# Softmax of a banded attention with negated scores, scales on ScalarE, one reciprocal for three tiles, and convolution taps ordered behind the minima

## The chip, the cores and the metric

One core of a Trainium2 chip runs the kernel. Its engines work side by side, each with a queue of its own that it works off in order: TensorE (PE, matrix products and transposes), VectorE (DVE), ScalarE (ACT), GpSimd (POOL) and SyncE (SP), which issues most of the DMAs. Semaphores between the queues say when an instruction may start. The metric is the time of the whole program on the device in microseconds, as the median of several executions.

## The reference

One layer of a streaming encoder, for 2048 prompt tokens and 64 sample tokens, with a model width of 1024 and 8 heads of 64:

```python
h = rms_norm(x, norm1_g) * (1 + sc1) + sh1
z = h @ w_in                          # GLU pair | q | k | v | two gates
u = glu_a * sigmoid(glu_b)
conv_out = conv_module(u, ...)        # depthwise conv of 31 taps, layer norm, swish, product
q, k = rms_norm(q), rms_norm(k)       # per head
s = einsum('bqhd,bkhd->bhqk', q, k) * 0.125 + rel_bias
s = where(mask, s, NEG_INF)           # own chunk of 64 and the 8 chunks before
o = einsum('bhqk,bkhd->bqhd', softmax(s, axis=-1), v)
merged = sigmoid(g_conv) * conv_out + sigmoid(g_attn) * (o @ w_attn_out)
x = x + gt1 * (merged @ w_o)
x = x + gt2 * swiglu_ffn(rms_norm(x, norm2_g) * (1 + sc2) + sh2)
```

The cached rows of the sample's keys, values and convolution inputs are read, and their new states are outputs. All is in float32.

## The kernel before

Float32 products are made of three products of parts: an operand is split into a high and a low part (whi and wlo for weights, hh and hl for activations, ph and pl for probabilities), so a row ps<-hh,whi is followed by ps<-hl,whi and ps<-hh,wlo.

The program has two phases. In phase 1 the 2112 tokens go through in four blocks (576 with the samples, then three of 512). Each block goes through the stages q, 0, k, 1, v, 2, 3 and g: projections to queries, keys and values; four stages of the GLU pair with the convolution of 128 channels each (`convolve`, L1158, whose 30 taps are a `scalar_tensor_tensor` each on VectorE, L1174, y<-u,wd,y in the rows); and the gates. The attention of a block needs its v, and runs beside the stages that follow: those of its own block and the first of the next one. Phase 2 (from about 1230 us) makes the gated merge, the output projection and the FFN in three blocks of tokens.

Attention works head by head (`attend`, L1371), 40 in all: 16 in block 0 (eight of the prompt, with four tiles of 128 queries and 128, 256, 384 and 512 keys, and between them eight of the samples, with one tile of 64 x 320), and eight in each later block, with four tiles of 128 x 640. Per tile: TensorE makes the scores into sc, of which there is one buffer in PSUM. `softmax_max` (L1270) adds the bias, multiplies by 0.125 and takes the maximum of each row, in one instruction on VectorE (in the order a row ISA pr,sm and a row ISA sm, in the trace CUSTOM_DVE_ANT_0 and its accumulator read), negates the maximum on VectorE, and ScalarE makes Exp with the sum. `softmax_scale` (L1285) takes the reciprocal on VectorE and multiplies the tile by it: on VectorE in blocks 0 to 2, on ScalarE in block 3 (`ON_ACT = (3,)`, L48). It is called for a tile when the next one's Exp has been written down. When all four are scaled, TensorE transposes the probabilities (ptp), ScalarE and VectorE split them into ph and pl, and TensorE multiplies them by the values into po; `finish_head` (L1313) adds two halves into o_p.

What sets the order: the code is written as generators on `Lane`s (L109), which a `Stream` (L162) steps on as TensorE's estimated load passes the time that each has asked for, as long as the load of VectorE and ScalarE isn't too far ahead:

```python
stream.lanes = [norm_lane, work, attn, tail, conv]    # L1476
yield free + PE_LAG, SCORE_ROOM                       # L1396, between two tiles
yield stream.when("act" if x in ON_ACT else "dve") + PE_LAG   # L1404, before the transposes
```

Behind that the compiler's own scheduler sorts the instructions once more by its estimates, so that the final order on an engine is not the order of the code. The operations of all engines go through one recording helper, so nearly all rows have its line (L104 before, L103 after); they are told apart by their tiles.

Of the kernel before, what the change touches and what calls it, by code (L numbers as in the profile page):

```python
# [8 lines left out]
F32 = mybir.dt.float32  # L9
F32R = mybir.dt.float32r  # L10
AF = mybir.ActivationFunctionType
ALU = mybir.AluOpType
# [4 lines left out]
P = 128  # L17
# [26 lines left out]
PE_LAG = 400.0  # L44
TURN_LAG = 2500.0
KN_LAG = 5000.0
X_LAG = 8000.0
ON_ACT = (3,)  # L48
ON_POOL = ()
# [8 lines left out]
SCORE_ROOM = {"dve": 2500}  # L58
# [525 lines left out]
def streaming_layer(ctx: ExitStack, tc: tile.TileContext, I, O):  # L584
    nc = tc.nc
    stream = Stream()
    pe, dve, act, gps = (
        Meter(e, n, stream) for e, n in ((nc.tensor, "pe"), (nc.vector, "dve"), (nc.scalar, "act"), (nc.gpsimd, "pool"))
    )
# [44 lines left out]
    wd = const.tile([P, 4, TAPS], F32, name="wd")  # L634
# [91 lines left out]
    wk = p1.enter_context(tc.tile_pool(name="wk", bufs=1))  # L726
# [201 lines left out]
    bias = wk.tile([P, 640], F32, name="bias")  # L928
# [203 lines left out]
    def glu(b, ct):  # L1132
# [23 lines left out]
        return u  # L1156

    def convolve(u, y, ct, b):  # L1158
        w = UW if b == 0 else HIST + QB
        n = w - HIST  # L1160
# [12 lines left out]
        for k in range(1, TAPS):  # L1173
            dve.scalar_tensor_tensor(y[:, ct, :n], u[:, k : k + n], wd[:, ct, k : k + 1], y[:, ct, :n], ALU.mult, ALU.add)  # L1174
            yield
# [93 lines left out]

    def softmax_max(ps, n, w, bias):  # L1270
        pr = wk.tile([P, 640], F32, tag="pr", name="pr", bufs=8)
        sm = wk.tile([P, 4], F32, tag="sm", name="sm", bufs=9)
        nb = ps.shape[1]
        stream.after("dve", "pe")
        dve.tensor_tensor_reduce(
            out=pr[:n, :w].rearrange("p (a b) -> p a b", a=nb), in0=ps, in1=bias.rearrange("p (a b) -> p a b", a=nb),
            scale=0.125, scalar=-3e38, op0=ALU.add, op1=ALU.max, accum_out=sm[:n, 0:1],
        )
        dve.tensor_scalar(sm[:n, 1:2], sm[:n, 0:1], -1.0, None, ALU.mult)
        free = stream.when("dve")  # L1280
        stream.after("act", "dve")
        act.activation(pr[:n, :w], pr[:n, :w], AF.Exp, bias=sm[:n, 1:2], accum_out=sm[:n, 2:3])
        return pr, sm, free, stream.when("act")

    def softmax_scale(pr, sm, n, w, on_act):  # L1285
        dve.reciprocal(sm[:n, 3:4], sm[:n, 2:3])
        if on_act:
            stream.after("act", "dve")
            act.activation(pr[:n, :w], pr[:n, :w], AF.Copy, scale=sm[:n, 3:4])
        else:  # L1290
            dve.tensor_scalar(pr[:n, :w], pr[:n, :w], sm[:n, 3:4], None, ALU.mult)

# [55 lines left out]

    order, loaded, now = [], {}, {"scored": -1, "finished": -1, "bias": None}

# [20 lines left out]
    def attend(i):  # L1371
        x, h = order[i]
        q0, nq, k0, nk = spans(x)
# [4 lines left out]
        (q2, kk), (_, bias), vnow = now["qk", i], now["bias"], now["v", i]  # L1378
        tiles = []
        for t in range(0, nq, P):  # L1380
            n = min(P, nq - t)
# [6 lines left out]
            else:  # L1388
# [3 lines left out]
                src, bs = ps[:n, 0:1, :w], bias[:n, 64:384][:, ::-1] if x == "s" else bias[:, :w][:, ::-1]  # L1392
            pr, sm, free, ready = softmax_max(src, n, w, bs)
            tiles.append((pr, sm, n, w))
            if t + P < nq:
                yield free + PE_LAG, SCORE_ROOM  # L1396
            else:
                fetch(i + 1)
                now["scored"] = i
            if t:  # L1400
                softmax_scale(*tiles[-2], x in ON_ACT)
        yield ready
        softmax_scale(*tiles[-1], x in ON_ACT)
        yield stream.when("act" if x in ON_ACT else "dve") + PE_LAG  # L1404
        while now["finished"] < i - 1:
# [676 lines left out]
```

## Time and profile before

| | us |
|---|---|
| median of three executions | 3047.6 (3043.95 to 3049.64) |
| the profiled execution | 3048.7 |
| its span, first to last instruction | 3046.9 |
| TensorE busy | 2936.2 |
| VectorE busy | 2043.0 |
| ScalarE busy | 1254.4 |
| GpSimd busy | 989.7 |
| mean granted TensorE clock | 0.987 |

In the rows, "out<-in" names tiles of the program and "x" the number of instructions in a row. In a timeline a row starts with its start and its length in us, and "[5.64 <-DVE sm]" is idle time of that engine ahead of it and what ended it. In a table of windows each engine's busy time stands before its number of instructions. In the groups of instructions "busy, mean ns of one" is followed by the idle time of the engine ahead of them. In the rows of waits the numbers are the total in us, how many, and the longest.

### The profile page before, as it was taken

How to read it: one execution, taken by the hardware profiler on the slowest of the kernel's cores; microseconds unless marked ns; L12 is line 12 of the kernel's file. 1: busy time of each engine (PE TensorE's matmuls, PEld its weight loads, DVE VectorE, ACT ScalarE, POOL GpSimd, SP SyncE). 2: the span in 40 equal slices, each digit the busy share in tenths (PEclk: the TensorE clock that was granted, in tenths of full speed). 3: DMA queues.
4: the chain of work that ended last, by engine and by line, in shares of the span. 5: the costliest groups of instructions: out<-in, count | busy, mean ns of one | idle time of the engine just before them, and what ended most of it. 6: DMA issues, size and time to landing. Idle time of an engine off the chain costs nothing. (4 is left out here: it accounts for less than half of the span.)

```text
span 3046.9 us, 44878 instructions
## 1 busy us (share of the span) xinstructions
PE 2936.2 (96%) x16259; PEld 2609.2 (86%) x16259; DVE 2043.0 (67%) x3826; ACT 1254.4 (41%) x2260; POOL 989.7 (32%) x617
## 2 busy tenths in 40 slices
PE   7989898999999999989999999999999999999998
PEld 4789777888878788878998989999999898999997
DVE  4797687877977895467666755655666756366567
ACT  2324432453245257364444424534444244333331
POOL 0200210101011102355677433247767341333331
PEclk9999998999999999999999999999999999999999
DMA  9789788887987788886444686445556965355554
GB/s 336 262 276 309 224 293 267 270 263 265 306 277 247 250 267 274 259 278 218 144 149 142 227 292 202 159 166 190 181 196 202 344 213 189 119 167 174 166 162 174
DMA packets 487084, 693.07 MB, mean 227 GB/s; under 512 B 38485, under 2 KB 316873, under 8 KB 486862
## 3 DMA queue, kind: packets, MB, share of 16 engines
q1 hardware_dynamic: 474581, 672.82, 67.2%
q10 hardware_dynamic: 12280, 17.39, 1.6%
q8 instruction: 128, 2.10, 0.3%
q14 instruction: 95, 0.77, 0.1%
HBM read 505.89 MB, written 184.19 MB: 226 GB/s over the span
## 5 line engine op out<-in xcount | busy, mean ns | idle before, releaser
L104 POOL TENSOR_TENSOR wlo<-wst,whi 128x1024 fp32r<-128x1024 f32 (+1 forms) x180 | 402.6, 2243 | 499.5 <-ACT whi L104 427.6
L104 PE MATMUL ps<-t,whi 128*128 128x384 f32 (+1 forms) x2112 | 505.8, 323 | 10.5 <-DVE t L104 4.8
L104 PE MATMUL pd<-whi,hid 128*128 128x512 f32 (+1 forms) x1400 | 450.3, 391 | 3.4 <-DVE acc L104 3.4
L104 ACT ACTIVATE whi<-wst 128x1024 fp32r<-128x1024 f32 (+1 forms) x269 | 262.0, 978 | 360.5 <-PE ps L104 120.1
L104 PE MATMUL ps<-b,whi 128*128 128x384 f32 (+1 forms) x1584 | 381.1, 326 | 11.4 <-DVE pw L104 4.0
L104 PEld LDWEIGHTS ps<-t,whi 128*128 128x128 f32 x2112 | 370.6, 189 | 18.6 <-ACT u L104 5.5
L104 DVE SCALAR_TENSOR_TENSOR y<-u,wd,y 128x512 f32<-128x512 f32 (+1 forms) x480 | 368.3, 771 | 6.5
L104 PE MATMUL ps<-hh,whi 128*128 128x512 f32 (+2 forms) x992 | 363.6, 367 | 0.0
L104 PE MATMUL ps<-hl,whi 128*128 128x512 f32 (+2 forms) x992 | 346.6, 349 | 0.0
L104 PE MATMUL ps<-hh,wlo 128*128 128x512 f32 (+2 forms) x992 | 346.0, 349 | 0.0
L104 DVE TENSOR_TENSOR acc<-acc,pd 128x512 f32<-128x512 f32 (+1 forms) x440 | 290.5, 684 | 80.4 <-PE pd L104 76.8
L104 PE MATMUL ps<-t,wlo 128*128 128x384 f32 (+1 forms) x1056 | 340.8, 323 | 0.0
L104 PEld LDWEIGHTS pd<-whi,hid 128*128 128x128 f32 (+1 forms) x1400 | 258.1, 184 | 64.7 <-DVE acc L104 6.9
L104 PEld LDWEIGHTS ps<-b,whi 128*128 128x128 f32 x1584 | 278.1, 189 | 14.7 <-DVE pw L104 4.3
L104 PE MATMUL pd<-wlo,hid 128*128 128x512 f32 (+1 forms) x700 | 273.7, 391 | 0.0
L104 PE MATMUL ps<-b,wlo 128*128 128x384 f32 (+1 forms) x792 | 257.1, 325 | 0.0
L104 POOL TENSOR_TENSOR r<-t,mhalf 128x8 f32<-128x8 f32 (+3 forms) x68 | 84.5, 1244 | 390.9 <-DVE t L104 368.0
L104 PEld LDWEIGHTS ps<-hh,wlo 128*128 128x128 f32 x992 | 187.9, 189 | 22.4
L104 POOL TENSOR_TENSOR wlo<-wup,whi 128x1024 fp32r<-128x1024 f32 (+1 forms) x64 | 138.3, 2162 | 208.8 <-ACT whi L104 176.5
L104 PEld LDWEIGHTS ps<-hh,whi 128*128 128x128 f32 x992 | 188.8, 190 | 18.7 <-issue 2.1
L104 PEld LDWEIGHTS ps<-hl,whi 128*128 128x128 f32 x992 | 188.8, 190 | 15.4 <-issue 1.7
L104 PEld LDWEIGHTS ps<-t,wlo 128*128 128x128 f32 x1056 | 199.3, 189 | 0.6
(217 smaller groups left out, 5725.5 us busy)
## 6 DMA issues: line engine op xcount, KB each, us to landing
whi<-w_din_h SPq DMA_DIRECT2D x72, 512.0 KB, 5.9
wlo<-w_din_l SPq DMA_DIRECT2D x72, 512.0 KB, 7.1
wst<-sum_d SPq DMA_DIRECT2D x131, 256.0 KB, 3.0
wmod<-in_w_ada SPq DMA_DIRECT2D x48, 512.0 KB, 8.5
sum_d<-ws SPq DMA_DIRECT2D x88, 256.0 KB, 2.4
wst<-in_w_ffn_in SPq DMA_DIRECT2D x85, 256.0 KB, 3.4
wst<-in_w_ffn_in SPq DMA_DIRECT2D x37, 512.0 KB, 5.4
wst<-in_w_in SPq DMA_DIRECT2D x36, 512.0 KB, 7.1
```

Source lines behind the costliest of these rows:

```text
L104: return f(*args, **kw)
```

## The change

Scores are kept negated: the scale is -0.125, the tile's extreme is a minimum, and Exp takes its input times -1 with the minimum as its bias, so that the separate negation is gone. The bias is added as before. One tile sm of 128 x 12 per head replaces one of 128 x 4 per tile of scores. The scale of every tile is a Copy on ScalarE; those of the first three tiles are written behind the fourth Exp, with one reciprocal over three columns, and the last has a reciprocal of its own; a sample head has one. The first tap that is written after a minimum is tied behind it on VectorE (`behind`, which uses the scheduler's `issue_after`).

```diff
@@ -1,4 +1,4 @@
-from contextlib import ExitStack
+from contextlib import ExitStack, nullcontext
 
 import concourse.bass as bass
 import concourse.tile as tile
@@ -45,7 +45,6 @@
 TURN_LAG = 2500.0
 KN_LAG = 5000.0
 X_LAG = 8000.0
-ON_ACT = (3,)
 ON_POOL = ()
 DMA_LAG = 4000.0
 OUT_LAG = 4000.0
@@ -1155,6 +1154,12 @@
         W.done()
         return u
 
+    def behind(one):
+
+        return tc.issue_after(one.ins) if one is not None else nullcontext()
+
+    now = {"scored": -1, "finished": -1, "bias": None}
+
     def convolve(u, y, ct, b):
         w = UW if b == 0 else HIST + QB
         n = w - HIST
@@ -1171,7 +1176,8 @@
         gps.tensor_copy(hist[:, ct], u[:, w - HIST : w])
         dve.tensor_scalar(y[:, ct, :n], u[:, :n], wd[:, ct, 0:1], bdw[:, ct : ct + 1], ALU.mult, ALU.add)
         for k in range(1, TAPS):
-            dve.scalar_tensor_tensor(y[:, ct, :n], u[:, k : k + n], wd[:, ct, k : k + 1], y[:, ct, :n], ALU.mult, ALU.add)
+            with behind(now.pop("least", None)):
+                dve.scalar_tensor_tensor(y[:, ct, :n], u[:, k : k + n], wd[:, ct, k : k + 1], y[:, ct, :n], ALU.mult, ALU.add)
             yield
 
     def conv_norm(y, c0, n, t0):
@@ -1267,28 +1273,29 @@
             free["columns"] = c1
 
 
-    def softmax_max(ps, n, w, bias):
+    def softmax_max(ps, n, w, bias, sm, j):
+
         pr = wk.tile([P, 640], F32, tag="pr", name="pr", bufs=8)
-        sm = wk.tile([P, 4], F32, tag="sm", name="sm", bufs=9)
         nb = ps.shape[1]
         stream.after("dve", "pe")
-        dve.tensor_tensor_reduce(
+        now["least"] = dve.tensor_tensor_reduce(
             out=pr[:n, :w].rearrange("p (a b) -> p a b", a=nb), in0=ps, in1=bias.rearrange("p (a b) -> p a b", a=nb),
-            scale=0.125, scalar=-3e38, op0=ALU.add, op1=ALU.max, accum_out=sm[:n, 0:1],
+            scale=-0.125, scalar=3e38, op0=ALU.add, op1=ALU.min, accum_out=sm[:n, j : j + 1],
         )
-        dve.tensor_scalar(sm[:n, 1:2], sm[:n, 0:1], -1.0, None, ALU.mult)
         free = stream.when("dve")
         stream.after("act", "dve")
-        act.activation(pr[:n, :w], pr[:n, :w], AF.Exp, bias=sm[:n, 1:2], accum_out=sm[:n, 2:3])
-        return pr, sm, free, stream.when("act")
-
-    def softmax_scale(pr, sm, n, w, on_act):
-        dve.reciprocal(sm[:n, 3:4], sm[:n, 2:3])
-        if on_act:
-            stream.after("act", "dve")
-            act.activation(pr[:n, :w], pr[:n, :w], AF.Copy, scale=sm[:n, 3:4])
-        else:
-            dve.tensor_scalar(pr[:n, :w], pr[:n, :w], sm[:n, 3:4], None, ALU.mult)
+        act.activation(pr[:n, :w], pr[:n, :w], AF.Exp, bias=sm[:n, j : j + 1], scale=-1.0, accum_out=sm[:n, 4 + j : 5 + j])
+        return pr, n, w
+
+    def softmax_scale(tiles, sm, a, b):
+
+        n = tiles[a][1]
+        stream.after("dve", "act")
+        dve.reciprocal(sm[:n, 8 + a : 8 + b], sm[:n, 4 + a : 4 + b])
+        stream.after("act", "dve")
+        for j in range(a, b):
+            pr, n, w = tiles[j]
+            act.activation(pr[:n, :w], pr[:n, :w], AF.Copy, scale=sm[:n, 8 + j : 9 + j])
 
     def load_qk(h, q0, nq, k0, nk):
         hp, i = divmod(h, 2)
@@ -1346,7 +1353,7 @@
             )
         return bias
 
-    order, loaded, now = [], {}, {"scored": -1, "finished": -1, "bias": None}
+    order, loaded = [], {}
 
     def attention(b):
 
@@ -1376,7 +1383,8 @@
         fetch_v(i)
         yield loaded[i]
         (q2, kk), (_, bias), vnow = now["qk", i], now["bias"], now["v", i]
-        tiles = []
+        tiles, nt = [], (nq + P - 1) // P
+        sm = wk.tile([P, 12], F32, tag="sm", name="sm", bufs=3)
         for t in range(0, nq, P):
             n = min(P, nq - t)
             ps = ps_a.tile([P, 2, 512], F32, tag="s", name="sc")
@@ -1390,18 +1398,17 @@
                 for d in range(2):
                     pe.matmul(ps[:n, 0, :w], q2[:, d, t : t + n], kk[:, :w], start=d == 0, stop=d == 1)
                 src, bs = ps[:n, 0:1, :w], bias[:n, 64:384][:, ::-1] if x == "s" else bias[:, :w][:, ::-1]
-            pr, sm, free, ready = softmax_max(src, n, w, bs)
-            tiles.append((pr, sm, n, w))
+            tiles.append(softmax_max(src, n, w, bs, sm, t // P))
             if t + P < nq:
-                yield free + PE_LAG, SCORE_ROOM
+                yield stream.when("dve") + PE_LAG, SCORE_ROOM
             else:
                 fetch(i + 1)
                 now["scored"] = i
-            if t:
-                softmax_scale(*tiles[-2], x in ON_ACT)
-        yield ready
-        softmax_scale(*tiles[-1], x in ON_ACT)
-        yield stream.when("act" if x in ON_ACT else "dve") + PE_LAG
+        if nt > 2:
+            softmax_scale(tiles, sm, 0, nt - 1)
+        yield stream.when("act")
+        softmax_scale(tiles, sm, nt - 1 if nt > 2 else 0, nt)
+        yield stream.when("act") + PE_LAG
         while now["finished"] < i - 1:
             yield lambda: now["finished"] == i - 1
         fetch_v(i + 1)
```

In instructions: VectorE loses 136 negations, 104 scales and 64 reciprocals and gains three wlo that GpSimd loses; ScalarE gains 104 Copies; the counts on TensorE and SyncE are the same. The order on every engine is the same up to the first head of attention and from the first rows of phase 2 on. Between them it differs at many places. Three follow.

VectorE at the first head of attention, before (y<-u,wd,y are taps, ISA pr,sm the tile with its maximum, sm<-sm the negation):

```order
L104 SCALAR_TENSOR_TENSOR y<-u,wd,y 128x606
L104 TENSOR_SCALAR cc<-pt 30x128
L104 SCALAR_TENSOR_TENSOR y<-u,wd,y 128x606 x5
L104 ISA pr,sm<-sc,bias 128x128
L104 ISA sm 128x1
L104 SCALAR_TENSOR_TENSOR y<-u,wd,y 128x606
L104 TENSOR_SCALAR sm<-sm 128x1
L104 ISA pr,sm<-sc,bias 128x256
L104 ISA sm 128x1
L104 SCALAR_TENSOR_TENSOR y<-u,wd,y 128x606
L104 TENSOR_SCALAR sm<-sm 128x1
L104 RECIPROCAL sm<-sm 128x1
```

and after:

```order
L103 TENSOR_SCALAR cc<-pt 30x128
L103 ISA pr,sm<-sc,bias 128x128
L103 ISA sm 128x1
L103 SCALAR_TENSOR_TENSOR y<-u,wd,y 128x606
L103 ISA pr,sm<-sc,bias 128x256
L103 ISA sm 128x1
L103 SCALAR_TENSOR_TENSOR y<-u,wd,y 128x606
L103 ISA pr,sm<-sc,bias 128x384
L103 ISA sm 128x1
L103 SCALAR_TENSOR_TENSOR y<-u,wd,y 128x606
L103 ISA pr,sm<-sc,bias 128x512
L103 ISA sm 128x1
```

The five taps ahead of the first maximum now stand behind it, one between each two minima, and the negations are gone.

TensorE at the last sample head of block 0 (q_5019 before, q_5011 after; ps are projections, po the products with the values), before:

```order
L104 MATMUL ps<-wlo,hh 128x512
L104 MATMUL ps<-whi,hl 128x512
L104 MATMUL sc<-kk,q_5019 64x320 x2
L104 MATMUL ptp<-ident,pr 128x64 x2
L104 MATMUL ptp<-ident,pr 64x64
L104 MATMUL ps<-whi,hh 128x512
L104 MATMUL ps<-wlo,hh 128x512
```

and after:

```order
L103 MATMUL ps<-whi,hh 128x512
L103 MATMUL ps<-wlo,hh 128x512
L103 MATMUL sc<-kk,q_5011 64x320 x2
L103 MATMUL ps<-whi,hl 128x512
L103 MATMUL po<-ph,vv 128x512
L103 MATMUL po<-pl,vv 128x512
L103 MATMUL ptp<-ident,pr 128x128
L103 MATMUL ps<-whi,hh 128x512
L103 MATMUL ps<-wlo,hh 128x512
```

The transposes followed the scores directly; now 25 projections and the eight products of the head before stand between them (the first are shown; the transposes of this head are 35 rows after its scores).

TensorE at the first head of block 3, before:

```order
L104 MATMUL ps<-hh,wlo 128x512
L104 MATMUL sc<-kk,q_10944 128x320 x4
L104 MATMUL ps<-hh,whi 128x512
L104 MATMUL ps<-hl,whi 128x512
L104 MATMUL ps<-hh,wlo 128x512
L104 MATMUL ps<-hh,whi 128x512
L104 MATMUL ps<-hl,whi 128x512
L104 MATMUL ps<-hh,wlo 128x512
L104 MATMUL sc<-kk,q_10944 128x320 x4
```

and after:

```order
L103 MATMUL pt<-ident,u 30x128
L103 MATMUL ps<-hh,whi 128x512
L103 MATMUL ps<-hl,whi 128x512
L103 MATMUL ps<-hh,wlo 128x512
L103 MATMUL sc<-kk,q_10722 128x320 x16
L103 MATMUL ptp<-ident,pr 128x128
L103 MATMUL ps<-hh,whi 128x512
L103 MATMUL ps<-hl,whi 128x512
L103 MATMUL ps<-hh,wlo 128x512
L103 MATMUL ptp<-ident,pr 128x128 x3
```

Six projections stood between each two tiles of scores; now the sixteen products of all four tiles stand in a row, and the first transpose stands right behind them.

## The prediction

> **What bounds the kernel now.** I read the page's busy shares and its chain first, then the busy time by stage, then the waits of TensorE, and last the timeline at the places where the longest of those waits stand. The page:
>
> ```profile
> PE 2936.2 (96%) x16259; PEld 2609.2 (86%) x16259; DVE 2043.0 (67%) x3826; ACT 1254.4 (41%) x2260; POOL 989.7 (32%) x617
> PE 40%; DVE 2%; DMA 1%; issue 0%; ACT 0%; POOL 0%; SPq 0%; DVEq 0%; ACTq 0%
> ```
>
> TensorE is busy for 96% of the span, and no other engine comes near it. A microsecond taken off VectorE (DVE) or put on ScalarE (ACT) moves the end only where TensorE waits for it. Two things can be won: TensorE's idle time, and time in which its clock is granted low. Attention runs from 193 to 1230 us; these are that stretch and the one behind it (columns: busy time of each engine, granted clock, DMA share, GB/s):
>
> ```profile
> 193.00:215.00 22.00, 13.76 (x72) 11.48 (x71) 20.16 (x46) 6.54 (x16) 0.70 (x1) 0.77 0.89 312
> 215.00:305.00 90.00, 89.74 (x662) 87.09 (x661) 69.61 (x159) 40.02 (x94) 2.50 (x7) 1.00 0.86 282
> 305.00:533.00 228.00, 204.18 (x1118) 166.53 (x1117) 166.12 (x396) 82.63 (x190) 35.47 (x33) 0.93 0.80 261
> 533.00:1142.00 609.00, 599.49 (x3242) 502.78 (x3241) 494.77 (x1015) 252.78 (x477) 68.66 (x61) 1.00 0.83 268
> 1142.00:1230.00 88.00, 84.09 (x452) 71.11 (x451) 49.94 (x114) 62.79 (x106) 18.06 (x11) 1.00 0.83 261
> 1230.00:3040.00 1810.00, 1777.26 (x9748) 1638.36 (x9748) 1101.77 (x1858) 748.37 (x1280) 836.98 (x470) 0.99 0.59 197
> ```
>
> Idle in attention: 8.2 + 0.3 + 23.8 + 9.5 + 3.9 = 45.7 us. Clock: 22 x 0.23 = 5.1 us and 228 x 0.07 = 16.0 us are lost in the first and third stretch. So some 67 us is all there is to win, and most of it lies in two short places. In the long stretch from 533 to 1142 us TensorE idles for 9.5 us of 609 although VectorE is 81% busy there. The waits of TensorE that touch this:
>
> ```profile
> PE sc L104 <- DVE sm L104: 13.0, 10, 5.6
> PE ps L104 <- ACT hh L104: 9.6, 4, 4.9
> PE ptp L104 <- DVE pr L104: 9.5, 6, 5.8
> ```
>
> Scores (sc) waiting for the maximum of the tile before, since there is one score buffer, and transposes of the probabilities (ptp) waiting for the scale, make 22.5 us, and one event each makes about half of its row.
>
> **The change, part by part.** The durations, from the groups by line and shape (busy, mean ns):
>
> ```profile
> L104 DVE TENSOR_SCALAR sm<-sm 128x1 f32<-128x1 f32 x128 | 18.8, 147 | 0.9
> L104 DVE RECIPROCAL sm<-sm 128x1 f32<-128x1 f32 x128 | 19.9, 157 | 23.2 <-ACT pr L104 22.7
> L104 DVE TENSOR_SCALAR pr<-pr,sm 128x640 f32<-128x640 f32 x64 | 39.5, 616 | 0.8
> L104 ACT ACTIVATE pr<-pr,sm 128x640 f32<-128x640 f32 x128 | 104.6, 827 | 101.9 <-DVE sm L104 100.5 <-ACT gate L104 0.8
> L104 ACT ACTIVATION_READ_ACCUMULATOR pr<-pr,sm 128x1 f32 x128 | 23.9, 187 | 0.0
> L104 DVE CUSTOM_DVE_ANT_0 pr<-sc,bias 128x640 f32<-128x640 f32 x96 | 78.6, 818 | 27.2 <-PE sc L104 22.3 <-DMA bias<-rb_d 4.1
> ...
> L104 DVE DVE_READ_ACCUMULATOR2_ANT sm<- 128x1 f32 x128 | 10.5, 82 | 0.0
> ```
>
> The negation: 136 instructions by 147 ns, 20 us off VectorE. The reciprocals: 64 fewer by 157 ns, 10 us. A reciprocal over three columns isn't in the trace; I take the 157 ns of one column, and three times that would still be 0.3 us on an engine that waits there anyway. The scales: 64 of 616 ns and 40 narrower ones, about 55 us off VectorE and, at 827 ns and less, about 70 us onto ScalarE, which goes from 41% to 43% of the span. A minimum in place of a maximum isn't in the trace either: the same instruction, scale and operands, so 818 ns; slower or faster by its accumulator read (82 ns) would be 136 x 0.08 = 11 us of VectorE either way, under the same cover as the rest. Three low parts of weights (wlo) move from GpSimd to VectorE: 3 x 1.22 us (row 203.06 below). All of this, some 80 us less on VectorE and 70 more on ScalarE, I cost at nothing in itself: TensorE's own queue of projections hides it. Where that cover is gone, the price is the length of the chain from score to transpose. So the sum goes place by place.
>
> On ScalarE the first three scales now stand behind the fourth Exp. From the last score of a head, the first transpose can go after minimum, Exp and one Copy: 0.82 + 0.08 + 0.83 + 0.83 = 2.6 us with nothing else in the queues, and with hops between engines about 2.75 (estimate); the last tile after 0.9 + 0.83 + 0.19 + 4 x 0.83 = 5.2 us. In the new order most heads have 4.3 to 11 us of other products in between (rows counted, at the pitches of the trace), against 2.7 to 6.7 before.
>
> *First head (193 us).*
>
> ```profile
> 193.90 0.41 PE L104 MATMUL sc<-kk,q 128*128 128x128 f32 x2
> 199.95 0.80 PE L104 MATMUL sc<-kk,q 128*128 128x256 f32 x2 [5.64 <-DVE sm L104]
> 201.27 1.01 PE L104 MATMUL sc<-kk,q 128*128 128x384 f32 x2 [0.53 <-DVE sm L104]
> 202.94 1.22 PE L104 MATMUL sc<-kk,q 128*128 128x512 f32 x2 [0.66 <-DVE sm L104]
> ...
> 205.27 0.69 PE L104 MATMUL ptp<-ident,pr 128*128 128x128 f32 x2 [0.90 <-DVE sm L104]
> 206.48 0.90 PE L104 MATMUL ptp<-ident,pr 128*128 128x128 f32 x3 [0.52 <-DVE pr L104]
> ...
> 195.31 4.37 DVE L104 SCALAR_TENSOR_TENSOR y<-u,wd,y 128x606 f32<-128x606 f32 x5
> 199.60 0.28 DVE L104 CUSTOM_DVE_ANT_0 pr<-sc,bias 128x128 f32<-128x128 f32 x1
> ...
> 203.06 1.22 DVE L104 TENSOR_TENSOR wlo<-wst,whi 128x1024 fp32r<-128x1024 f32 x1
> ```
>
> The scores were there at 194.3, and VectorE ran five taps (4.37 us) ahead of the maximum. After the change the taps stand behind it, and 13, 7 and 3 projections stand between the scores. TensorE idled 8.25 us here; I leave 3.3 (some 2 before the first transpose, the rest where a tap delays a minimum): 5 us won. The clock lost 5.1 us in this window; half of it comes back: 7.5 in all.
>
> *Last sample head of block 0 (474 us).*
>
> ```profile
> 473.82 0.39 PE L104 MATMUL ps<-whi,hl 128*128 128x512 f32 x1
> 474.05 0.45 PE L104 MATMUL sc<-kk,q 128*64 128x320 f32 x2
> 480.34 0.55 PE L104 MATMUL ptp<-ident,pr 64*128 64x64 f32 x3 [5.84 <-DVE pr L104]
> ...
> 475.72 1.53 DVE L104 SCALAR_TENSOR_TENSOR y<-u,wd,y 128x512 f32<-128x512 f32 x2
> 477.16 0.47 DVE L104 CUSTOM_DVE_ANT_0 pr<-sc,bias 64x320 f32<-64x320 f32 x1
> ...
> 480.50:489.50 9.00, 9.00 (x26) 7.15 (x26) 4.71 (x10) 0.97 (x4) 1.24 (x2) 0.50 0.41 134
> ```
>
> Nothing stood between its scores and its transposes, while taps stood between each two of its steps. Afterwards 25 full-width projections (0.23 us apart, as 473.82 to 474.05 shows, so 5.8 us) and eight products of the head before (above 1 us) stand there, and the chain, under 3 us, fits. Won: 5.84 us, and 9 x 0.5 = 4.5 of clock: 10.3.
>
> The other waits for sm and pr make 22.5 less 7.4 (the 0.90 above is no part of it) and 5.8: 9.3 us in eleven events. The first head of block 1 keeps two bare scores in the new order; the others are spread. I take 3 won, between 0 and 9.
>
> *The step to block 1 (365 to 400 us).*
>
> ```profile
> 372.11 0.49 PE L104 MATMUL ps<-whi,hh 128*128 128x512 f32 x1 [2.65 <-ACT hh L104]
> 374.13 0.63 PE L104 MATMUL ps<-whi,hh 128*128 128x512 f32 x1
> 382.73 0.79 PE L104 MATMUL ps<-whi,hh 128*128 128x512 f32 x1 [4.95 <-ACT hh L104]
> ...
> 379.57 0.69 DVE L104 TENSOR_TENSOR kn<-kn,r 128x512 f32<-128x512 f32 x1 [3.85 <-POOL r L104]
> ...
> 373.06 4.87 POOL L104 TENSOR_TENSOR y<-y,s 128x512 f32<-128x512 f32 x4 [2.00 <-DVE s L104]
> ```
>
> Projections wait for hh, which waits for h on VectorE, which stands behind a kn that waits for GpSimd (POOL), where r stands behind four y. Nothing in the diff touches this, but the order does: the four y now come ahead of the first wide r. The 9.6 us of such waits and a share of the clock of that stretch (16.0 less 4.5 leaves 11.5) are open. Ends: 14 us won if all goes, 4 lost if new waits come (the 3.85 us once more). I take 6, nearest to the 4.95 row with a little clock.
>
> *New: first head of block 3.* Its sixteen score products now stand in a row; before, six projections stood between each two tiles. Each of three tiles waits for a minimum (0.82 + 0.08 and a hop, 1.0), and the first transpose waits 2.75: 5.9 us idle. The clock is the open part: at 372.11 a wait of 2.65 us was followed by products of 0.63 us where 0.39 is usual (473.82), so I add 3, two thirds of what the 5.84 us wait cost. Ends 5 and 11; taken 9 lost.
>
> The Trainium skill, in "TensorE: Matmul & The Clock Gate", section "Part 1: The HAM clock gate", puts the fall of the clock behind an idle window of about 3.4 us; by that rule none of these waits alone lowers it, and this loss would be 6 and the sum 3 better. The trace disagrees at 372.11 (2.65 us).
>
> *New: last head.*
>
> ```profile
> 1230.10 0.90 PE L104 MATMUL ps<-cin,whi 128*128 128x320 f32 x2 [1.41 <-DVE o_p L104]
> ```
>
> Before, projections stood between its transposes, and the join to phase 2 cost 1.4 us. Now all projections are used up before its last scores: 2.75 us to the first transpose, four scales in a row on ScalarE (5.2 us), and only behind those on its queue the copies of the transposes. TensorE has only 20 transposes and 16 products for that. Estimate: 5 us more idle and 1.5 of clock, 6.5 lost, ends 3 and 10.
>
> Heads with little between (three late ones in block 0, some in blocks 1 to 3 with 5 to 6 us against 5.2 and other work on ScalarE): 4.5 lost, ends 0 and 12.
>
> Behind 1240 us the order of every engine is unchanged: nothing. DMA triggers are the same in number; the next head's q and k load is still issued after a head's last score.
>
> Sum: 7.5 + 10.3 + 3 + 6 - 9 - 6.5 - 4.5 = 6.8 us won. The profiled execution took 3048.7 us (1.8 more than its span): 3041.9. It lies 1.1 above the median of three runs, so 3041 us for the median.
>
> **The rivals.**
>
> *Slower: ScalarE's queue sets the transposes.* In 40 heads the scales stand behind the fourth Exp and whatever copies, gates and casts come there. For it: the two drained heads above, and ScalarE at 63 of 88 us in the last stretch before the change. Against: TensorE idles 9.5 us in 609 with four steps on VectorE in the same chain. It decides from about 7 us for the chain (5.2 and two more ScalarE instructions), where half the heads of blocks 1 to 3 run short. At 1 us for each of those 24 heads the loss is 24 in place of 4.5: 3060 us.
>
> The Trainium skill, "ScalarE: Activation LUTs", section "Rules for kernel authors", gives multiplications to VectorE and not ScalarE; by that rule the move of the scales is a loss, and the rows agree on the price of one (827 against 616 ns).
>
> *No change.* The bare places only move: block 3's first head and the last head take what the first head and the sample head give, and the step to block 1 stays as it is (6 less): 3047 us. For it: all the idle time is where the order puts it, and the change re-draws the order without aiming at it. Against: the two events given up are the longest of their rows.
>
> *Much faster.* The step to block 1 clears wholly (14) and the last head and the thin ones cost half (5.5): 7.5 + 10.3 + 3 + 14 - 9 - 5.5 = 20 us, 3027 us. For it: 80 us less on VectorE, 81% busy from 533 on. Against: TensorE hardly waited there.
>
> **How the numbers follow.** About 0.2%, 6.1 us, is what a measurement of this kernel can tell from no change. The forecast has 0.45; its own range, 3033 to 3047, has its ends where the step to block 1 gives 14 us or nothing. The bound of "faster" lies at 3041.5, inside it, and the better end is the farther one (8 against 6), so 0.28 of it counts as faster and 0.17 as no change. Much faster has 0.14, no change 0.17 (0.02 of it past the bound on the slow side), slower 0.24. Faster: 0.28 + 0.14 = 0.42; same: 0.17 + 0.15 = 0.32; slower: 0.24 + 0.02 = 0.26. The range reaches from just past the much faster case to just past the slower one: 3026 to 3061.
>
> **What would show it.** Right: no wait above 2.5 us at the first head, none at the last sample head and a full clock behind it; ScalarE near 1325 us, VectorE near 1960 us busy. At the first head of block 3, three waits of sc for sm near 1 us and one of ptp for ScalarE's pr near 2.7 us; at the join to phase 2 more than 5 us. Wrong: waits of ptp for ScalarE's pr in many heads of blocks 1 to 3 (slower), or hh waits of 10 us and more again at the step to block 1.

## The result

The changed kernel is slower: 3067.2 us in the median of four runs (3064.6 to 3069.0), against 3048.6 us before (3044.0 to 3050.9, four runs). The ratio is 1.006, with a 95% interval of 1.0047 to 1.0073. The forecast was 3041 us with a range up to 3061. The profiled execution shown below took 3067.9 us, its span 3066.2 us.

The page of the changed kernel, busy time by engine:

```profile
PE 2942.3 (96%) x16259; PEld 2610.2 (85%) x16259; DVE 1994.3 (65%) x3525; ACT 1315.5 (43%) x2364; POOL 978.3 (32%) x614
```

VectorE lost 49 us and ScalarE gained 61. TensorE, the bound, is busy for 6 us longer and the span is 19 us longer. Where that lies, from the windows up to and from the join of the two phases, first of the kernel before, then of the changed one:

```profile
0.00:1230.00 1230.00, 1158.95 (x6511) 970.85 (x6511) 937.53 (x1963) 506.02 (x980) 152.77 (x147) 0.98 0.84 273
1230.00:3047.00 1817.00, 1777.26 (x9748) 1638.36 (x9748) 1105.48 (x1864) 748.37 (x1280) 836.98 (x470) 0.99 0.59 196
```

```profile
0.00:1250.00 1250.00, 1167.19 (x6512) 975.25 (x6513) 882.00 (x1659) 567.57 (x1085) 150.16 (x147) 0.98 0.82 269
1250.00:3066.00 1816.00, 1775.07 (x9748) 1634.92 (x9748) 1112.33 (x1866) 747.88 (x1280) 828.13 (x467) 0.99 0.59 197
```

Phase 2 takes 1816 to 1817 us in both. Phase 1 takes 20 us longer with the same matrix products. Its stretches in the changed kernel, to be read against the six rows of the prediction:

```profile
193.00:215.00 22.00, 19.02 (x121) 17.33 (x121) 14.64 (x30) 9.35 (x21) 2.69 (x3) 0.92 0.86 289
215.00:305.00 90.00, 86.52 (x633) 83.64 (x632) 76.26 (x142) 48.31 (x112) 8.19 (x14) 1.00 0.90 299
305.00:533.00 228.00, 208.85 (x1151) 169.41 (x1150) 156.06 (x329) 92.13 (x210) 29.48 (x26) 0.95 0.82 271
533.00:1142.00 609.00, 585.81 (x3145) 490.55 (x3144) 434.45 (x808) 287.20 (x524) 63.27 (x60) 0.99 0.80 259
1142.00:1260.00 118.00, 109.95 (x584) 93.53 (x583) 76.89 (x137) 72.25 (x123) 19.58 (x12) 0.97 0.78 239
```

In the first and the third stretch TensorE idles 9.9 us less (5.3 and 4.7) and has the better clock (0.92 for 0.77, 0.95 for 0.93). From 215 to 305 us it idles 3.2 us more. From 533 to 1142 us, where it idled 9.5 us before, it idles 23.2, and its clock, 1.00 before, is 0.99: the trace has it at 0.5 from 853.3 to 860.1, from 969.3 to 972.7 and from 1082.0 to 1088.8 us, which is 8.5 us lost. VectorE is busy there for 60 us less. So the kernel won early and lost late. What TensorE waits for now (total us, times, longest):

```profile
PE pm L103 <- POOL s L103: 13.0, 4, 7.2
PE sc L103 <- DVE sm L103: 11.5, 12, 3.3
PE ptp L103 <- ACT pr L103: 10.1, 5, 3.4
PE pt L103 <- DVE x_t L103: 8.2, 5, 2.7
PE ps L103 <- DVE t L103: 6.6, 4, 2.4
PE ps L103 <- ACT hh L103: 6.4, 4, 3.6
```

The first row is new: pm is the product that sums the 512 channels of the convolution's output for its layer norm (`conv_norm`, behind the taps), and it waits for s, which GpSimd adds up from the four y tiles. It waits once in each block; its longest wait, 7.2 us, is in block 2, at 856 us. The other large ones are the first head of block 3 and the last head of attention:

```profile
856.08 2.08 PE L103 MATMUL pm<-s,ones 128*128 128x512 f32 x2 [7.17 <-POOL s L103]
...
968.37 0.50 PE L103 MATMUL ps<-whi,hh 128*128 128x512 f32 x1 [3.59 <-ACT hh L103]
...
1077.88 0.84 PE L103 MATMUL sc<-kk,q 128*128 128x320 f32 x4 [0.93 <-DVE sm L103]
1079.65 0.85 PE L103 MATMUL sc<-kk,q 128*128 128x320 f32 x4 [0.93 <-DVE sm L103]
1081.43 0.98 PE L103 MATMUL sc<-kk,q 128*128 128x320 f32 x4 [0.93 <-DVE sm L103]
1085.01 0.47 PE L103 MATMUL ptp<-ident,pr 128*128 128x128 f32 x1 [2.60 <-ACT pr L103]
...
1236.11 0.85 PE L103 MATMUL sc<-kk,q 128*128 128x320 f32 x4 [0.97 <-DVE sm L103]
1240.37 3.03 PE L103 MATMUL ptp<-ident,pr 128*128 128x128 f32 x13 [3.41 <-ACT pr L103]
1249.87 0.56 PE L103 MATMUL ps<-cin,whi 128*128 128x320 f32 x2 [1.41 <-DVE o_p L103]
```

### The profile page after: what moved, and what is told of

It is laid out like the page before. It is cut to its first block, busy times and chain, and to the rows that moved or that the text cites. A ratio compares the mean times of both kernels' runs of the same rounds, so it can differ in the third digit from the quotient of the medians.

```text
span 3066.2 us, 44681 instructions
## 1 busy us (share of the span) xinstructions
PE 2942.3 (96%) x16259; PEld 2610.2 (85%) x16259; DVE 1994.3 (65%) x3525; ACT 1315.5 (43%) x2364; POOL 978.3 (32%) x614
## 5 line engine op out<-in xcount | busy, mean ns | idle before, releaser
L103 POOL TENSOR_TENSOR wlo<-wst,whi 128x1024 fp32r<-128x1024 f32 (+1 forms) x177 | 394.5, 2235 | 476.7 <-ACT whi L103 434.3
L103 PE MATMUL ps<-t,whi 128*128 128x384 f32 (+1 forms) x2112 | 505.5, 323 | 11.6 <-DVE t L103 5.5
L103 ACT ACTIVATE pr<-pr,sm 128x640 f32<-128x640 f32 (+4 forms) x272 | 195.2, 745 | 150.6 <-DVE sm L103 148.8
```

The source lines that it names most:

```text
L103: return f(*args, **kw)
```

## The experiments

Each kernel was timed against the kernel before on the same chip. The rows come from several batches on different chips, in which the kernel before took 3047.3 to 3048.6 us in the median, so a difference between two rows carries about 1 us.

| kernel | us | ratio to before | 95% interval |
|---|---|---|---|
| changed kernel | 3067.2 | 1.0060 | 1.0047 to 1.0073 |
| e1_untied: changed, without the tie | 3070.2 | 1.0066 | 1.0050 to 1.0082 |
| e2_tied: before, with the tie alone | 3042.6 | 0.9978 | 0.9967 to 0.9990 |
| e3_scale_each: changed, scales and reciprocals one by one | 3048.5 | 0.9998 | 0.9987 to 1.0009 |
| e6_norm_later: changed, layer-norm sum 8 us later | 3045.0 | 0.9988 | 0.9979 to 0.9998 |
| late_b2: changed, that sum later in block 2 alone | 3043.8 | 0.9987 | 0.9978 to 0.9996 |
| d3_each: changed, scales one by one in block 3 alone | 3054.0 | 1.0019 | 1.0010 to 1.0028 |
| late_b2_d3: the last two together | 3033.0 | 0.9952 | 0.9939 to 0.9965 |
| late_b2_d3_untied: that, without the tie | 3036.3 | 0.9963 | 0.9951 to 0.9976 |
| late_d3: sum later in all blocks, block 3 one by one | 3039.2 | 0.9968 | 0.9955 to 0.9980 |
| s_alone: before, all scales on ScalarE | 3054.1 | 1.0023 | 1.0013 to 1.0033 |
| n_alone: before, negated scores alone | 3043.2 | 0.9984 | 0.9975 to 0.9993 |
| tn: before, negated scores and tie | 3040.3 | 0.9978 | 0.9966 to 0.9990 |

### Is it the tie or the deferral?

The new wait stands behind the taps, so the tie of taps behind minima was the first suspect (theory A). The rival was the deferral of the scales behind the fourth Exp (theory B).

**e1_untied**, the changed kernel without the tie:

```diff
     def behind(one):
-        return tc.issue_after(one.ins) if one is not None else nullcontext()
+        return nullcontext()
```

> The changed kernel without the tie of taps behind the minima; negated scores, scales on ScalarE behind the fourth Exp and the shared reciprocal stay. Theory A (the tie holds the whole serial chain of taps behind a minimum that waits for its scores, so the convolution ends late and the sums of its layer norm make TensorE wait): the waits of pm for s, 13.0 us in the changed kernel, fall below 3 us, and the time comes to about 3052 us. Theory B (the deferral of the scales is the cause, by where it puts the other work of TensorE): the pm waits stay above 8 us, the first head of block 3 and the last head stay drained (sc and ptp waits of 5 to 6 us each), and the time stays at 3062 to 3070 us.

It took 3070.2 us, and the pm waits are gone. So both theories missed: A had the wait right and the time wrong; B had the drained heads right and the time almost (3070 was its upper end), and the wait wrong. The trace shows why. In both kernels the sum stands 12 products behind the score tile that precedes it. The changed kernel there, VectorE, then GpSimd:

```profile
847.00 0.82 DVE L103 CUSTOM_DVE_ANT_0 pr<-sc,bias 128x640 f32<-128x640 f32 x1
847.74 0.08 DVE L103 DVE_READ_ACCUMULATOR2_ANT sm<- 128x1 f32 x1
847.74 2.33 DVE L103 SCALAR_TENSOR_TENSOR y<-u,wd,y 128x512 f32<-128x512 f32 x3
849.98 0.16 DVE L103 RECIPROCAL sm<-sm 128x1 f32<-128x1 f32 x1
850.10 4.69 DVE L103 SCALAR_TENSOR_TENSOR y<-u,wd,y 128x512 f32<-128x512 f32 x6
...
854.93 1.09 POOL L103 TENSOR_TENSOR s<-s,y 128x512 f32<-128x512 f32 x1 [18.07 <-DVE y L103]
```

And without the tie, VectorE, GpSimd, TensorE:

```profile
847.89 1.54 DVE L103 SCALAR_TENSOR_TENSOR y<-u,wd,y 128x512 f32<-128x512 f32 x2
849.35 0.17 DVE L103 RECIPROCAL sm<-sm 128x3 f32<-128x3 f32 x1
849.43 0.80 DVE L103 CUSTOM_DVE_ANT_0 pr<-sc,bias 128x640 f32<-128x640 f32 x1
...
849.57 1.10 POOL L103 TENSOR_TENSOR s<-s,y 128x512 f32<-128x512 f32 x1 [23.86 <-DVE sm L103]
...
851.60 1.02 PE L103 MATMUL pm<-s,ones 128*128 128x512 f32 x2
```

The 30 taps of a channel tile are one chain, each reading the y of the tap before. The minimum that a tap is tied to stands ahead of all that are left. In the changed kernel nine taps (7.0 us) stand behind the fourth minimum; without the tie the last tap ends as that minimum starts, the sum is there at 850.7, and TensorE passes it at 851.6 without a wait. From 840 to 960 us idle time and lost clock fall from 10.6 to 1.2 us. The untied kernel loses more than that at the places for which the tie was made (there, in the stretches 193 to 215 and 400 to 533 us, they rise from 18 to 30 us): its first head waits 3.2 us and the first head of block 1 5.9. And the wait for hh at 968 us and the bare first head of block 3 are still there, though pm no longer waits ahead of them:

```profile
198.09 0.79 PE L103 MATMUL sc<-kk,q 128*128 128x256 f32 x2 [3.22 <-DVE sm L103]
...
517.01 1.44 PE L103 MATMUL sc<-kk,q 128*128 128x320 f32 x4 [5.94 <-DVE sm L103]
...
962.95 0.79 PE L103 MATMUL ps<-whi,hh 128*128 128x512 f32 x1 [3.60 <-ACT hh L103]
...
1074.26 1.07 PE L103 MATMUL sc<-kk,q 128*128 128x320 f32 x4 [1.87 <-DVE sm L103]
...
1082.84 0.47 PE L103 MATMUL ptp<-ident,pr 128*128 128x128 f32 x1 [2.60 <-ACT pr L103]
```

**e2_tied**, the kernel before with the tie alone:

```diff
-            dve.scalar_tensor_tensor(y[:, ct, :n], ...)
+            with behind(now.pop("least", None)):
+                dve.scalar_tensor_tensor(y[:, ct, :n], ...)
...
-        dve.tensor_tensor_reduce(
+        now["least"] = dve.tensor_tensor_reduce(
```

> The kernel before with the tie of taps behind the maxima alone. Theory A: pm waits of 7 to 13 us appear and the time is 3055 to 3062 us. Theory B: no pm wait above 2 us, the first head of block 3 and the last head as before, the wait of 5.6 us at the first head gone, and the time 3040 to 3048 us.

3042.6 us, 0.22% faster than before. The tie doesn't cost by itself: pm waits are 3.5 us in three places here, none above 1.4, and the 5.64 us wait at the first head has become 0.98. In this order the same sum stands 41 products later on TensorE than in the changed kernel: counted in the traces it is the 4612th product, against the 4571st (the 4611th before), and it waits 1.2 us. So the 7.2 us need both, the late taps and an early place of the sum.

**e3_scale_each**, the changed kernel with the scales one by one and a reciprocal for each:

```diff
-        if nt > 2:
-            softmax_scale(tiles, sm, 0, nt - 1)
+            if t:
+                softmax_scale(tiles, sm, t // P - 1, t // P)
         yield stream.when("act")
-        softmax_scale(tiles, sm, nt - 1 if nt > 2 else 0, nt)
+        softmax_scale(tiles, sm, nt - 1, nt)
```

> The changed kernel with the scales on ScalarE written one by one, each when the next tile's Exp has been written (as before), and a reciprocal for each; the tie and the negated scores stay. Theory A: the pm waits stay (13 us) and only the drained heads go (some 12 us with their clock): 3053 to 3058 us. Theory B: pm waits below 2 us, no sc or ptp wait above 2 us at the first head of block 3 and the last head, no wait at the last sample head of block 0: 3035 to 3045 us.

3048.5 us: the whole loss is gone, the gain doesn't come. The pm waits are 2.9 us, the first head of block 3 and the last head have projections again (1.4 us between its scores, 8.2 us ahead of the transposes of the last head, by the order). This is theory B's picture without its gain; scores wait 8.5 us in seven places for the DMA of kk here, which they do for 0.7 us in the changed kernel. The sum of block 2 is now TensorE's 4621st product; without the tie it stayed the 4571st. So the early place comes with the deferral of the scales, and the late taps with the tie.

### The place of one sum

**e6_norm_later** asks for the sum 8 us later, by the planner's due time:

```diff
             gps.tensor_tensor(s[:, :n], s[:, :n], yv[:, ct], ALU.add)
-        yield stream.when("pool") + PE_LAG
+        yield stream.when("pool") + PE_LAG + 8000.0
         pm = total()
```

> The changed kernel with the first sum of the convolution's layer norm asked for 8 us later in the planner (8000 more in the due time behind the three additions on GpSimd), all else as changed. If the place of that sum in TensorE's queue is the whole of the pm loss: pm waits gone, 13 us and 3 us of clock won, about 3051 us. If TensorE only meets VectorE's late taps at another place: other waits of like size (kn, hh, ptp) and 3060 us or more.

3045.0 us, 22 us less than the changed kernel and more than the 16 that were expected. The pm waits are 0.5 us in all. The wait of 3.6 us for hh at 968 and the bare first head of block 3 are gone with them, which the expectation did not have. Since the order changes from the first block on, the next run confines it.

**late_b2** does so for the layer norm of block 2 alone, so that TensorE's order up to 850 us is the changed kernel's:

```diff
-        yield stream.when("pool") + PE_LAG
+        yield stream.when("pool") + PE_LAG + (8000.0 if t0 == 1088 else 0.0)
```

> The changed kernel with the first sum of the layer norm asked for 8 us later in block 2 alone. Up to that sum (850 us) the order on TensorE is the changed kernel's, so what differs is behind it. Theory C (one early sum costs twice: 7.2 us of wait with its clock at 856 us, and behind it the order in which the first head of block 3 stands drained, 6 us of waits and 2 of clock): both go, the last head stays drained: 3067 less 7 to 9 less 6 to 8, 3050 to 3054 us. Theory D (the late taps of VectorE are the limit there and TensorE only waits elsewhere): 3060 us or more.

3043.8 us: this one place costs 23.4 us of the 3067.2. The windows from 840 us on, of the changed kernel, then of this run:

```profile
840.00:960.00 120.00, 112.83 (x625) 96.81 (x625) 73.36 (x151) 71.12 (x134) 13.60 (x14) 0.97 0.74 234
960.00:1060.00 100.00, 94.56 (x462) 77.90 (x461) 78.52 (x136) 37.23 (x64) 13.26 (x10) 0.98 0.72 232
1060.00:1142.00 82.00, 76.37 (x388) 63.83 (x387) 54.94 (x101) 36.88 (x68) 2.90 (x4) 0.96 0.80 265
```

```profile
840.00:960.00 120.00, 118.96 (x662) 101.84 (x662) 79.24 (x168) 78.29 (x145) 16.37 (x16) 1.00 0.80 245
960.00:1060.00 100.00, 98.64 (x488) 81.76 (x487) 79.80 (x133) 33.65 (x61) 13.32 (x11) 1.00 0.80 276
1060.00:1142.00 82.00, 82.00 (x442) 70.16 (x441) 67.94 (x121) 44.87 (x81) 1.60 (x2) 1.00 0.86 266
```

In each of the three, idle time goes (6.1, 4.1 and 5.6 us) and so does the low clock (3.4, 1.7 and 3.4 us lost by the trace's record of it): 24.4 us, which is the measured difference but for 1. Some 9.5 of it lie at the sum and 14.9 behind it. So theory C is right, and its price was low: beside the sum and the first head of block 3 the place also brings the hh wait at 968, which the theory left out. What lies behind the sum follows from its place and not from its wait: without the tie pm did not wait, and both were there. That the first head of block 3 is bare in the one order and covered in the other, though nothing was changed there, shows that the order behind a moved product is drawn anew; the rule by which it is drawn was not followed further.

### The scales behind the fourth Exp, in block 3

**late_b2_d3** adds to the run before, for block 3 alone, the scales one by one:

```diff
+            if t and x == 3:
+                softmax_scale(tiles, sm, t // P - 1, t // P)
-        if nt > 2:
+        if nt > 2 and x != 3:
             softmax_scale(tiles, sm, 0, nt - 1)
```

> As the run before, and in block 3 alone the scales are written one by one (each when the next tile's Exp is written) with a reciprocal each. If the scales behind the fourth Exp are what drains the last head: no wait of ptp above 1 us there, some 6 us below the run before, 3044 to 3048 us. If not, the same time as the run before.

3033.0 us, 10.8 less, and the fastest of all: 0.48% under the kernel before (0.35 to 0.61%). At the join of the phases (late_b2, then this run):

```profile
1216.82 3.46 PE L103 MATMUL ptp<-ident,pr 128*128 128x128 f32 x15 [3.41 <-ACT pr L103]
1226.50 0.56 PE L103 MATMUL ps<-cin,whi 128*128 128x320 f32 x2 [1.40 <-DVE o_p L103]
```

```profile
1214.90 0.56 PE L103 MATMUL ps<-cin,whi 128*128 128x320 f32 x2 [1.46 <-DVE o_p L103]
```

The transposes of the last head no longer wait, and phase 2 starts 11.6 us earlier. That is more than the 6 expected: the wait of 3.41 us, one of 0.97 ahead of it and 3.4 us of lost clock (0.5 from 1216.0 to 1222.8 us in late_b2) make 7.8; the rest was not assigned.

**d3_each** has the scales one by one in block 3 and the early sum of block 2:

> The changed kernel with the scales written one by one in block 3 alone; the early sum of block 2 stays. Theory C: the 7.2 us wait of pm and the drained first head of block 3 stay, the last head is covered: 3067 less 5 to 7, about 3061 us. If the deferral of the scales drained the first head of block 3 as well: about 3053 us.

3054.0 us, 13.2 less than the changed kernel where 5 to 7 or 14 were expected. The 7.19 us of pm and the three waits of 0.93 us at the first head of block 3 are still there, while its transposes no longer wait 2.60 us. So the deferral had cost at both ends of block 3, but did not bare the scores of its first head. The four kernels with and without each of the two edits (3067.2, 3043.8, 3054.0, 3033.0) give 23.4 and 13.2 us apart and 34.2 together: two causes that nearly add up (36.6).

### What the parts are worth

**late_b2_d3_untied**, the fastest kernel without the tie:

> The fastest kernel so far (changed kernel, first sum of block 2's layer norm 8 us later, scales one by one in block 3) without the tie of taps. If the tie is worth what it wins where taps stood ahead of minima (first head, first head of block 1): waits of sc of 3 and 6 us come back there with their low clock, 3043 to 3052 us. If the tie only costs: 3033 us or less.

3036.3 us, 3.3 more; the intervals of the two overlap. The waits of 3.0 and 5.9 us at the first heads of blocks 0 and 1 are back as expected, for less time than they should cost, since other waits went, among them those of pm in blocks 0 and 1 (2.7 and 1.5 us). The tie is worth little here, at most a few us.

**s_alone**, the kernel before with ScalarE for all scales:

```diff
-ON_ACT = (3,)
+ON_ACT = (0, "s", 1, 2, 3)
```

> The kernel before with all scales on ScalarE (as it had them in block 3), written one by one; no tie, the negation stays. If the move of the scales to ScalarE costs by itself: ptp waits for ScalarE's pr in many heads and 3055 us or more. If it costs nothing: no such wait above 2 us, TensorE's 5.6 us wait at the first head stays, that of 5.8 us at the last sample head goes since its order has products there: 3038 to 3050 us.

3054.1 us, 0.23% slower, but not by the mechanism of the expectation: ptp waits for ScalarE's pr are 2.1 us in two places. What is long in it is the wait of scores for VectorE at the first heads of blocks 0 and 1 (5.59 and 7.79 us), the latter from 2.49 in the kernel before. So the price is again one of order; that it belongs to the move as such isn't shown.

**n_alone**, the kernel before with a minimum and without the negation:

```diff
-            scale=0.125, scalar=-3e38, op0=ALU.add, op1=ALU.max, accum_out=sm[:n, 0:1],
+            scale=-0.125, scalar=3e38, op0=ALU.add, op1=ALU.min, accum_out=sm[:n, 0:1],
         )
-        dve.tensor_scalar(sm[:n, 1:2], sm[:n, 0:1], -1.0, None, ALU.mult)
...
-        act.activation(pr[:n, :w], pr[:n, :w], AF.Exp, bias=sm[:n, 1:2], accum_out=sm[:n, 2:3])
+        act.activation(pr[:n, :w], pr[:n, :w], AF.Exp, bias=sm[:n, 0:1], scale=-1.0, accum_out=sm[:n, 2:3])
```

> The kernel before with negated scores and a minimum alone, so that the 136 negations on VectorE are gone; scales, reciprocals and taps as before. If VectorE's 20 us lie under TensorE: within 6 us of before but for what the new order does at the first head and the last sample head; that one has 3.9 us of products between scores and transposes in this order, so its 5.8 us wait shrinks below 2.5: 3038 to 3047 us. If the negation lies on TensorE's path in many heads: 3030 us or less.

3043.2 us, 0.16% faster: inside the first expectation. The last sample head has no wait above 1.2 us left; the first head keeps 5.25 us, and the first head of block 1 grew to 8.79.

**tn**, negation and tie together on the kernel before:

> The kernel before with the negated scores and the tie, no scale moved and no reciprocal shared. If the gains of the two add (tie 6, negation 0 to 9): 3034 to 3042 us. If the order of the whole decides and not the parts: anything from 3036 to 3055 us, and then the difference lies in a few waits above 2 us.

3040.3 us, ratio 0.9978 as with the tie alone. Both expectations hold this number, so it tells only that the 0.16% and 0.22% of the two do not add.

**late_d3**, the sum later in all blocks and block 3 one by one:

> The changed kernel with the first sum of the layer norm 8 us later in all blocks and the scales one by one in block 3. The last head is covered in this order (4.8 us of projections between the last scores and the first transpose), the last sample head has 2 us only: 3032 to 3040 us, near the kernel with block 2 alone (3033). If the sums of blocks 0, 1 and 3 cost as that of block 2 did, 3028 us or less.

3039.2 us, ratio 0.9968. Moving the sums of the other blocks as well gained nothing: the time is 6 us above late_b2_d3, with a wait of 4.55 us for hh at 365 us that the latter has not. What those sums cost by themselves isn't shown, since the order changes with them.

## Why the prediction was wrong

Taken by its own steps, with three more windows of the changed kernel and then one of the kernel before:

```profile
365.00:400.00 35.00, 29.72 (x140) 24.32 (x139) 22.86 (x58) 18.51 (x42) 7.37 (x6) 0.90 0.66 228
...
1076.00:1092.00 16.00, 10.49 (x47) 8.11 (x48) 7.48 (x16) 8.69 (x16) 0.00 (x0) 0.79 0.91 256
1234.00:1256.00 22.00, 16.02 (x87) 14.16 (x88) 11.29 (x23) 12.55 (x21) 0.00 (x0) 0.84 0.37 123
```

```profile
365.00:400.00 35.00, 26.52 (x111) 21.05 (x112) 24.00 (x59) 13.56 (x27) 12.45 (x9) 0.85 0.51 169
```

- **What bounds the kernel** was right: TensorE's idle time and clock in phase 1, and nothing in phase 2.
- **First head: 7.5 us won.** Right. The window idles 3.0 us for 8.2, and its clock rose from 0.77 to 0.92 (3.4 us): 8.7 us. The first transposes wait 2.08 us where 2 were left for them.
- **Last sample head: 10.3 won.** Right at its place: TensorE has no wait above 0.25 us between the one that ends at 441.9 and the one that ends at 509.8 us. Those two (2.6 us for part_l, which is new, and 3.3 us at the first head of block 1, for 2.5 before) take part of it back.
- **The step to block 1: 6 won.** Right at its place and wrong as a term. From 365 to 400 us TensorE is busy 29.7 us for 26.5 and its clock is 0.90 for 0.85, which is 5 us. But new waits for a minimum and for ssq and part_l, two more tiles that VectorE writes, before and behind it (1.4 us at 425, 1.8 at 323, 2.6 at 442) took it back: without the sample head's 5.8 the idle time of the whole stretch rose by 1.2.
- **First head of block 3: 9 lost.** Right to the mechanism and the number: three waits of 0.93 and one of 2.60, 5.4 us idle, and a clock of 0.79 in the 16 us from 1076, 3.4 us: 8.8. The clock fell after waits none of which was above 2.6 us, as the prediction took it from the 2.65 us wait and against the rule of the Trainium skill ("TensorE: Matmul & The Clock Gate", "Part 1: The HAM clock gate") that it cited.
- **Last head: 6.5 lost.** Right: 5.8 us of waits from 1236 on, 1.4 of them also there before, and a clock of 0.84 from 1234 to 1256, 3.4 us lost, where the kernel before lost 1.7 at its join (0.5 from 1230.1 to 1233.5 us): 6.1 more. Undoing its cause in block 3 gave 10.8 to 13.2 us, since that also took away the low clock of the join and, in d3_each, part of the loss at the first head.
- **Other waits for sm and pr: 3 won; heads with little between: 4.5 lost.** Neither shows as a term. Transposes wait for ScalarE's pr in two thin heads only (0.5 us at 220, 1.5 at 344), so the 4.5 was too much; new waits of scores for a minimum took the 3.
- **The cover of VectorE's and ScalarE's work: nothing.** This step failed. "All of this ... I cost at nothing in itself: TensorE's own queue of projections hides it" was said of durations, and of the tie only the gain was priced, taps that step back for a minimum. It was not asked who waits for the taps. Behind the last tap stand GpSimd's sum and TensorE's pm, whose place in TensorE's queue was in the new order already (40 products earlier than before). A chain of nine taps by 0.75 us behind a minimum and a sum that comes 12 products behind a score tile could be read there. pm waits 13.0 us in four places; from 840 to 1060 us, with its longest wait, the hh wait at 968 and the low clock behind each, TensorE loses 17.7 us where the kernel before lost 6.1 and the sum had nothing.

The rows of the kernel before for the late stretches:

```profile
840.00:960.00 120.00, 116.58 (x649) 99.27 (x648) 87.66 (x197) 60.87 (x119) 15.23 (x14) 1.00 0.81 257
960.00:1060.00 100.00, 97.31 (x482) 80.57 (x481) 86.28 (x155) 31.13 (x56) 13.97 (x10) 1.00 0.75 251
1060.00:1142.00 82.00, 81.61 (x431) 68.88 (x430) 73.00 (x153) 43.56 (x78) 4.29 (x5) 1.00 0.88 278
```

Place by place, the difference of the two kernels in TensorE's idle time and lost clock (the clock from the trace's record, unrounded):

| stretch | forecast, us | measured, us |
|---|---|---|
| first head, 193 to 215 us | 7.5 won | 8.7 won |
| 215 to 365 us | nothing | 5.7 lost |
| step to block 1, 365 to 400 us | 6 won | 4.9 won |
| last sample head, 400 to 533 us | 10.3 won | 5.7 won |
| 533 to 840 us | nothing | 2.0 lost |
| sum of block 2 and hh, 840 to 1060 us | nothing | 11.6 lost |
| first head of block 3, 1060 to 1142 us | 9 lost | 8.7 lost |
| last head, from 1142 us to 10 us behind the join | 6.5 lost | 5.7 lost |
| other waits and thin heads | 1.5 lost | in the rows above |
| together | 6.8 won | 14.4 lost |

The profiled execution is 19.2 us longer (3067.9 for 3048.7). Of the 4.8 us that the table leaves, 2.4 lie before 193 us, where TensorE's order is the same, and 2.4 are not assigned. The 23.4 us of late_b2 can't be set against the forecast whole, since the first head of block 3, which the sum already held at 9, is in them. That late_b2 comes to 3043.8, near the forecast of 3041, is luck in part for the same reason: the head for which 9 were taken off is covered there.

Of the signs that the prediction named, all but VectorE's busy time (1994 us for 1960) came true, and the time still fell outside the range: they were signs of the places that the sum had. The rival "slower" named ScalarE's queue in many heads; ptp waits for ScalarE's pr in five places only, 10.1 us in all, two of them at the drained heads. It would have given a similar time for another reason.

## What to carry to other kernels

When an instruction is held back, price what waits for the whole chain behind it, not only what it makes room for: here a tap held for a minimum cost nothing at the minimum, and 7 us at a sum two engines further on. Where a planner places a consumer by an estimate of its producer, a change that shifts the producer must be checked at every such place; one due time, moved by 8 us in one block, changed the time by 23.4 us, the four edits together by 18.6. More than half of the 23.4 came from the order behind the sum and not from its wait, so a wait's own length is not its price in such a planner. And a saving of 49 us on an engine that is not the bound shows up only through the order that it causes, so the idle places of the bound are to be compared in the old and the new order one by one.

## What the hardware showed that was not expected

- Short waits lower the clock: three waits of 0.93 us and one of 2.60 within 8 us left a granted clock of 0.79 over 16 us, and over the three windows of late_b2 lost clock was 8.5 us beside 15.8 us of idle time. In the traces of the two kernels the record of the clock has only the values 1 and 0.5, and each low stretch lasts 3.41 us or two or three times that, but for the last, which the end of the program cuts off. The one from 1082 us follows 3.4 us in which TensorE was busy for 46% and no idle stretch was longer than 0.93 us; that points to the busy share of such a stretch and not to one long wait:

```profile
1078.60:1082.00 3.40, 1.55 (x9) 1.17 (x8) 1.66 (x4) 1.70 (x5) 0.00 (x0) 1.00 0.94 372
1082.00:1088.80 6.80, 4.20 (x14) 3.04 (x14) 3.10 (x7) 4.13 (x8) 0.00 (x0) 0.50 0.72 169
```

- Removing VectorE instructions frees less than their durations. The durations of VectorE's instructions add up to 71 us less (2220 to 2150), while its busy time fell by 49 us, since an instruction can start while the one ahead is still ending: the minimum at 847.00 us takes 0.82, and the next two rows start at 847.74.
- A reciprocal of 128 x 3 takes 169 ns for the 157 of 128 x 1, and a minimum 819 ns for the 818 of a maximum.
